# Gated delta rule: block transposes on VectorE for the inverse's transpose, and last products in runs of one shape

## The chip, the cores and the metric

The kernel runs on one core of a Trainium2 chip, whose engines work side by side and wait for each other by semaphores: TensorE (PE; its weight loads are PEld), VectorE (DVE), ScalarE (ACT), GpSimd (POOL) and SyncE (SP), which issues the loads. The metric is the device time of one execution in microseconds, as the median of the runs; lower is better.

## The reference

Two decoder blocks on 512 tokens of width 1024 (float32). The first mixes tokens in four ways at once, each with four heads of 64: softmax attention with forgetting, a gated delta rule, and two gated linear attentions; then come a feed-forward layer with a short convolution, and a second block with a convolution mixer, latent attention and two more feed-forward layers. The change lies in the gated delta rule alone, whose costly step is the solution of triangular systems, one for each head and chunk of 64 tokens:

```python
m = jnp.where(strict, jnp.einsum('bhnrd,bhnsd->bhnrs', kb, k) * decay, 0.0)
t_mat = m + jnp.eye(c, dtype=m.dtype)
w = lax.linalg.triangular_solve(t_mat, kb * jnp.exp(G)[..., None], left_side=True, lower=True, unit_diagonal=True)
u = lax.linalg.triangular_solve(t_mat, v * beta[..., None], left_side=True, lower=True, unit_diagonal=True)
```

## The kernel before

All of the first block's mixing is one stage, some 400 of 1861 us. Its dense products (29 tiles of the input projection, 8 of the output projection, each in 24 matmuls of 128x512, since every operand is split in two parts) run between four kinds of mixing work, which are written as generators in three lanes: the two linear attentions, the gated delta rule (`gdn`, once for heads 0 and 1 and once for heads 2 and 3), and softmax attention. The order of TensorE's instructions is written out by a planner, `conduct` (line 758). It keeps a clock of its own, to which each product adds a set cost (`mm`, line 704; `tr`, line 711), and resumes a generator when the time it yielded is over: `yield LV` waits 1.0 us of that clock. Where no generator is due, it issues the next step of a dense tile. The other engines take their instructions in an order that the framework derives from the program's.

`gdn` works on four chunks of 128 tokens at once (tiles of 128x512, chunk by chunk) and inverts the triangular matrices by doubling. X is the inverse so far, XT its transpose; both start from blocks of two rows. XT is made on VectorE (lines 1110 and 1111). X comes from it by four TensorE transposes into PSUM and a copy on ScalarE (line 1121, behind a `yield LV`), for each of the two heads (j). Then follow six levels (line 1125), in which the blocks grow from 2b = 4 to 128 rows. A level takes four steps, each behind a `yield LV`:

- for each head, Y = mask x (MR X): four matmuls (line 1134) and a VectorE multiplication (line 1137);
- for each head, `pp` = XT Y (line 1140), added to X on VectorE (line 1141), and `pt` = Y XT (line 1142), which a VectorE update brings into XT (line 1143). `up` and `lo` select the columns, 64 of each 128.

`mm4` makes four matmuls into one PSUM tile of the lane, and the lane has two such tiles (`gps`, line 642). Behind the levels comes one correction step (lines 1149 to 1160), and then the last products of the pair (lines 1163 to 1173): u from XT and v, w from k and XT, in 16 matmuls, of which every second has an output of 64 partitions that starts at partition 0 or 64. These are float32, so that each is two records in the profile. Two ScalarE copies bring u and w out, and a scan over the four chunks uses them.

In the rows below, TensorE's instructions stand under the lines of two helpers, 705 (matmul) and 712 (transpose), as output<-moving,stationary operand: `gps<-gx,gmr` is the Y product, `gps<-gy,gxt` is `pp`, `gps<-gxt,gy` is `pt`, `gps<-mlac,gxt` the transposes of XT, `gps<-mlac,gv` those of v, `gps<-gvn,gmr` and `gps<-gmr,gke` the last products, and `mm<-` a dense product.

Of the kernel before, what the change touches and what calls it, by code (L numbers as in the profile page):

```python
# [14 lines left out]
ACTF = mybir.ActivationFunctionType  # L15
# [630 lines left out]
LA, LV, LP = 0.68, 1.0, 1.5  # L646
# [17 lines left out]
class Mix(Mla):  # L664
# [371 lines left out]
    def gdn(self, p):  # L1036
        nc = self.nc
# [7 lines left out]
        f1 = lambda t: t.bitcast(F32)  # L1045
        G, GL = h4(self.G[:, 0:16]), h4(self.G[:, 16:32])
        eG, eGL = h4(self.eG[:, 0:16]), self.eG[:, 16:32]
        ke, ko, vn = self.b("gke"), self.b("gko"), self.b("gvn")
# [5 lines left out]
        for i, y in enumerate((k, q)):  # L1054
# [4 lines left out]
                out=ss[:, 8 - 8 * i : 16 - 8 * i], in_=sq.rearrange("p (a d) -> p a d", d=64), axis=AX.X, op=ALU.add  # L1059
# [12 lines left out]
        nk = self.s1(8, "gnk", 2)  # L1072
        nc.vector.tensor_tensor(out=nk, in0=ss[:, 8:16], in1=rr[:, 8:16], op=ALU.mult)
        yield 0.0
        MT, MR, AT, X, XT = [], [], [], [], []
        for j in range(2):
            rows = slice(64 * j, 64 * j + 64)
# [9 lines left out]
            for c in range(4):  # L1087
                nc.scalar.activation(
                    out=e[:, c * 128 : c * 128 + 128], in_=gp[:, c * 128 : c * 128 + 128], func=ACTF.Exp,
# [4 lines left out]
            for c in range(4):  # L1094
                cs = slice(c * 128, c * 128 + 128)
# [5 lines left out]
            for c in range(4):  # L1101
                cs = slice(c * 128, c * 128 + 128)
# [13 lines left out]
        tp = self.to_tokens(v)  # L1116
        nc.vector.tensor_tensor(out=d4(vn), in0=d4(tp), in1=b64(h2(nk)), op=ALU.mult)
        for j in range(2):
            yield LV
            x = self.b("gx", F32R, bufs=2)  # L1120
            nc.scalar.activation(out=x, in_=self.to_tokens(f1(XT[j])), func=ACTF.Copy)
            X.append(x)
        self.over.add(f"gdn{p}.kv")
        Y = self.gy
        for lv in range(6):
            b = 2 << lv
            up = lambda t: t.rearrange("p (n j) -> p n j", j=2 * b)[:, :, :b]
            lo = lambda t: t.rearrange("p (n j) -> p n j", j=2 * b)[:, :, b:]
            if lv == 2:
                for mt in MT:  # L1130
                    nc.gpsimd.tensor_tensor(out=c4(mt), in0=c4(mt), in1=bc(self.strict), op=ALU.mult)
            for j in range(2):
                yield LV
                yp = self.mm4(MR[j], X[j], up)
                c4b = lambda t: t.rearrange("p (c n j) -> p c n j", c=4, j=2 * b)[:, :, :, :b]
                gm = self.gmask[:, lv].rearrange("p (n j) -> p n j", j=b).unsqueeze(1).to_broadcast([128, 4, 64 // b, b])
                nc.vector.tensor_tensor(out=c4b(Y[j]), in0=c4b(yp), in1=gm, op=ALU.mult)
            for j in range(2):
                yield LV
                pp = self.mm4(XT[j], Y[j], up)  # L1140
                nc.vector.tensor_tensor(out=up(X[j]), in0=up(f1(X[j])), in1=up(pp), op=ALU.add)
                pt = self.mm4(Y[j], XT[j], lo)
                nc.vector.scalar_tensor_tensor(
                    out=lo(XT[j]), in0=lo(pt), scalar=self.grow[:, lv : lv + 1], in1=lo(f1(XT[j])),
                    op0=ALU.mult, op1=ALU.add,
                )
# [15 lines left out]
        yield LV  # L1162
        up = self.pst()
        wp = self.pst()
        for c in range(4):
            for j in range(2):
                cs = slice(c * 128, c * 128 + 128)
                hs = slice(c * 128 + j * 64, c * 128 + j * 64 + 64)
                self.mm(up[:, hs], XT[j][:, cs], vn[:, hs])
                self.mm(wp[64 * j : 64 * j + 64, cs], ke[:, hs], XT[j][:, cs])  # L1170
        u, w = vn, ke
        nc.scalar.activation(out=u, in_=up, func=ACTF.Copy)
        nc.scalar.activation(out=w, in_=wp, func=ACTF.Copy, scale=-1.0)
# [3 lines left out]
        for c in range(4):  # L1177
            cs = slice(c * 128, c * 128 + 128)
            if st is None:
                vt = u[:, cs]  # L1180
            else:
# [8 lines left out]
                    out=h64(os_[:, cs]), in0=h64(qp[:, 0:128]),  # L1190
# [3 lines left out]
            if c < 3:  # L1194
# [4 lines left out]
                for j in range(2):  # L1199
# [3 lines left out]
                    else:  # L1203
                        col = 4 * c + 2 * p + j
                        nc.vector.scalar_tensor_tensor(
                            out=new[rs, rs], in0=st[rs, rs], scalar=eGL[rs, col : col + 1], in1=kp[rs, rs],
# [4 lines left out]
            for j in range(2):  # L1211
                hs = slice(j * 64, j * 64 + 64)
# [475 lines left out]
```

## Time and profile before

| What | Value |
|---|---|
| median of the runs | 1862.54 us |
| lowest run | 1862.07 us |
| profiled execution | 1862.47 us |
| its span, first to last instruction | 1860.8 us |
| PE busy | 1822.3 us, 98% |
| PEld busy | 1501.5 us, 81% |
| DVE busy | 1050.7 us, 56% |
| ACT busy | 737.8 us, 40% |
| POOL busy | 194.4 us, 10% |

The span is the time from the first to the last instruction; the execution has some 1.7 us around it. Matmuls overlap each other in their pipeline, so that the duration of one is longer than the distance to the next; distances between starts tell what an instruction costs. PEclk is the granted share of TensorE's full clock, where 1.00 is 2.4 GHz and 0.50 is 1.2 GHz. A chain of waits is followed back from the last instruction of a stretch, at each step to what released it.

### The profile page before, as it was taken

What the parts mean: (1) busy time and instruction counts of PE and PEld (TensorE: products, weight loads), DVE (VectorE), ACT (ScalarE), POOL (GpSimd) and SP (SyncE); (2) the same over time, 40 slices, a digit from 0 to 9 for tenths busy, and PEclk for the clock granted to TensorE, in tenths of its full rate; (3) what the DMA queues carried; (4) which work ended last, traced back from release to release, by engine and by line L of the source; (5) the groups of instructions that cost most, each with busy time, mean ns of one, the idle gap of its engine ahead of it and who ended that gap; (6) DMA issues with size and microseconds to landing.
All of it is one profiled execution on the core that took longest, in us unless ns stands there. A gap on an engine that the chain in (4) does not pass through costs nothing.

```text
span 1860.8 us, 22057 instructions
## 1 busy us (share of the span) xinstructions
PE 1822.3 (98%) x8609; PEld 1501.5 (81%) x8609; DVE 1050.7 (56%) x1627; ACT 737.8 (40%) x1138; POOL 194.4 (10%) x225
## 2 busy tenths in 40 slices
PE   8999999999999999999999999999999999999997
PEld 6787887778888888888888888888777888888886
DVE  7875985767777633455564444333876454444323
ACT  6543544544444422322343233322577333232322
POOL 1510502210000001011200000011011200000001
PEclk9999999999999999999999999999999999999999
DMA  4111101332323333323232323333222222323332
GB/s 167 57 35 46 46 35 35 106 101 91 102 93 100 90 100 94 102 91 102 92 106 92 102 91 102 94 94 97 71 60 74 79 96 97 102 91 99 94 94 76
DMA packets 53223, 162.61 MB, mean 87 GB/s; under 512 B 6528, under 2 KB 13184, under 8 KB 53120
## 3 DMA queue, kind: packets, MB, share of 16 engines
q1 hardware_dynamic: 52992, 161.21, 27.2%
q8 instruction: 67, 1.10, 0.3%
q14 instruction: 36, 0.29, 0.0%
q10 hardware_dynamic: 128, 0.01, 0.0%
HBM read 157.78 MB, written 2.10 MB: 86 GB/s over the span
## 4 chain that ended last, share of the span: by engine, by line
PE 85%; DVE 9%; ACT 3%; issue 1%; POOL 1%; DMA 0%; SPq 0%; DVEq 0%; ACTq 0%; POOLq 0%
PE mm L125 24%; PE mm L127 24%; PE mm L126 24%; PE mm L705 6%; PE gps L705 3%; PE lps L705 1%; PE fps L705 1%; DVE lbd L1310 1%; ACT wh L111 1%; DVE wl L112 1%; DVE lat L1361 1%; PE ps L577 1%; DVE ptl L112 0%; PE ps L165 0%; DVE nm L580 0%
## 5 line engine op out<-in xcount | busy, mean ns | idle before, releaser
L111 ACT ACTIVATE wh<-raw 128x1024 fp32r<-128x1024 f32 (+3 forms) x308 | 308.6, 1003 | 762.6 <-PE mm L126 463.5
L125 PE MATMUL mm<-xh,wh 128*128 128x512 f32 x1336 | 521.8, 391 | 0.4 <-ACT xh L173 0.4
L126 PE MATMUL mm<-xl,wh 128*128 128x512 f32 x1336 | 520.7, 390 | 0.5 <-DVE xl L174 0.5
L127 PE MATMUL mm<-xh,wl 128*128 128x512 f32 x1336 | 519.9, 389 | 0.0
L112 DVE TENSOR_TENSOR wl<-raw,wh 128x1024 fp32r<-128x1024 f32 (+3 forms) x300 | 361.0, 1203 | 224.8 <-ACT wh L111 221.6
L126 PEld LDWEIGHTS mm<-xl,wh 128*128 128x128 f32 x1336 | 250.8, 188 | 54.9 <-DVE xl L174 1.4
L125 PEld LDWEIGHTS mm<-xh,wh 128*128 128x128 f32 x1336 | 250.8, 188 | 53.7 <-issue 1.0
L127 PEld LDWEIGHTS mm<-xh,wl 128*128 128x128 f32 x1336 | 250.8, 188 | 51.9 <-issue 0.2
L125 PE MATMUL mm<-hidh,wh 128*128 128x512 f32 (+1 forms) x614 | 236.7, 386 | 0.0
L127 PE MATMUL mm<-hidh,wl 128*128 128x512 f32 (+1 forms) x614 | 235.3, 384 | 0.0
L126 PE MATMUL mm<-hidl,wh 128*128 128x512 f32 (+1 forms) x614 | 233.8, 381 | 0.0
L127 PEld LDWEIGHTS mm<-hidh,wl 128*128 128x128 f32 x614 | 115.4, 188 | 24.2
L126 PEld LDWEIGHTS mm<-hidl,wh 128*128 128x128 f32 x614 | 115.4, 188 | 23.6
L705 PE MATMUL mm<-xh,wh 128*128 128x512 f32 x291 | 127.7, 439 | 6.6 <-ACT xh L173 5.8
L125 PEld LDWEIGHTS mm<-hidh,wh 128*128 128x128 f32 x614 | 115.5, 188 | 21.9 <-ACT wh L111 0.2
L705 PE MATMUL mm<-xh,wl 128*128 128x512 f32 x291 | 116.0, 398 | 1.6 <-DVE wl L112 1.6
L705 PE MATMUL mm<-xl,wh 128*128 128x512 f32 x291 | 116.1, 399 | 0.4 <-DVE xl L112 0.4
L278 DVE TENSOR_TENSOR u<-mm,rb 128x512 f32<-128x512 f32 x44 | 30.4, 691 | 141.2 <-PE mm L127 141.2
L158 POOL TENSOR_TENSOR z<-z,sq 128x512 f32<-128x512 f32 x31 | 50.9, 1643 | 556.6 <-ACT sq L156 518.9
L274 DVE TENSOR_TENSOR u<-mm,rb 128x512 f32<-128x512 f32 x44 | 30.4, 691 | 90.9 <-PE mm L127 90.8
L111 ACT ACTIVATE hidh<-s 128x512 fp32r<-128x512 f32 x66 | 41.8, 633 | 88.6 <-DVE s L255 57.5
L705 PEld LDWEIGHTS mm<-xh,wh 128*128 128x128 f32 x291 | 56.1, 193 | 18.8 <-ACT xh L173 6.3
(434 smaller groups left out, 2089.2 us busy)
## 6 DMA issues: line engine op xcount, KB each, us to landing
raw<-in_w_a_dram SPq DMA_DIRECT2D x52, 512.0 KB, 3.3
raw<-in_w_b_dram SPq DMA_DIRECT2D x52, 512.0 KB, 3.4
raw<-in_w_up_dram SPq DMA_DIRECT2D x44, 512.0 KB, 3.3
raw<-in_w_in_dram SPq DMA_DIRECT2D x28, 512.0 KB, 3.3
raw<-in_conv_w_in_dram SPq DMA_DIRECT2D x24, 512.0 KB, 3.3
raw<-in_w_down_dram SPq DMA_DIRECT2D x16, 448.0 KB, 3.4
raw<-in_w_a_dram SPq DMA_DIRECT2D x16, 448.0 KB, 3.3
raw<-in_w_b_dram SPq DMA_DIRECT2D x16, 448.0 KB, 3.3
```

The lines of the kernel that those rows point to most:

```text
L111: nc.scalar.activation(out=h, in_=src, func=ACTF.Copy)
L112: (eng or nc.vector).tensor_tensor(out=l, in0=src, in1=h.bitcast(F32), op=ALU.subtract)
L125: nc.tensor.matmul(out=ps, lhsT=h, rhs=xh, start=(k == 0), stop=False)
L126: nc.tensor.matmul(out=ps, lhsT=h, rhs=xl, start=False, stop=False)
L127: nc.tensor.matmul(out=ps, lhsT=l, rhs=xh, start=False, stop=(k == kt - 1))
L158: eng.tensor_tensor(out=acc, in0=acc, in1=sq, op=ALU.add)
L274: nc.vector.tensor_tensor(out=g, in0=ps, in1=r, op=ALU.mult)
L278: nc.vector.tensor_tensor(out=g, in0=ps, in1=r, op=ALU.mult)
L577: nc.tensor.matmul(out=ps[:, :n], lhsT=l[:, qs], rhs=r[:, :n], start=(i == 0), stop=False)
L705: self.nc.tensor.matmul(out=out, lhsT=lhsT, rhs=rhs, start=start, stop=stop)
L1310: nc.vector.tensor_tensor(out=bd[rows, :, h].rearrange("p c (n j) -> p c n j", j=b), in0=c4(q)[rows], in1=c4(d)[rows], op=ALU.mult)
L1361: nc.vector.copy_predicated(out=at.rearrange("p c (n j) -> p c n j", j=2 * b)[:, :, :, b:], mask=self.lmask[:, lv - 1].rearrange("p (n j) ...
```

## The change

Three edits, all in `gdn`. The first X of each head comes from XT by a VectorE transpose of the whole 128x512 tile and a ScalarE copy that rounds it; the yields before it go. This transpose turns each 32x32 block within itself, which is the transpose of a matrix that has nothing outside its diagonal blocks of up to 32 rows. In the levels with 2b up to 32, the first four of six, the same helper makes XT from the new X, in place of the product `pt` and its update; the last two levels stay. The last products are issued as eight for u and then eight for w.

```diff
@@ -1072,6 +1072,12 @@
         nk = self.s1(8, "gnk", 2)
         nc.vector.tensor_tensor(out=nk, in0=ss[:, 8:16], in1=rr[:, 8:16], op=ALU.mult)
         yield 0.0
+        def flipped(dst, src):
+
+            t = self.t(tag="s")
+            nc.vector.transpose(out=t, in_=f1(src))
+            nc.scalar.activation(out=dst, in_=t, func=ACTF.Copy)
+
         MT, MR, AT, X, XT = [], [], [], [], []
@@ -1116,9 +1122,8 @@
         tp = self.to_tokens(v)
         nc.vector.tensor_tensor(out=d4(vn), in0=d4(tp), in1=b64(h2(nk)), op=ALU.mult)
         for j in range(2):
-            yield LV
             x = self.b("gx", F32R, bufs=2)
-            nc.scalar.activation(out=x, in_=self.to_tokens(f1(XT[j])), func=ACTF.Copy)
+            flipped(x, XT[j])
             X.append(x)
@@ -1139,6 +1144,10 @@
                 yield LV
                 pp = self.mm4(XT[j], Y[j], up)
                 nc.vector.tensor_tensor(out=up(X[j]), in0=up(f1(X[j])), in1=up(pp), op=ALU.add)
+                if 2 * b <= 32:
+
+                    flipped(XT[j], X[j])
+                    continue
                 pt = self.mm4(Y[j], XT[j], lo)
@@ -1162,12 +1171,14 @@
         yield LV
         up = self.pst()
         wp = self.pst()
-        for c in range(4):
-            for j in range(2):
-                cs = slice(c * 128, c * 128 + 128)
-                hs = slice(c * 128 + j * 64, c * 128 + j * 64 + 64)
-                self.mm(up[:, hs], XT[j][:, cs], vn[:, hs])
-                self.mm(wp[64 * j : 64 * j + 64, cs], ke[:, hs], XT[j][:, cs])
+        blocks = [
+            (slice(c * 128, c * 128 + 128), slice(c * 128 + j * 64, c * 128 + j * 64 + 64), j)
+            for c in range(4) for j in range(2)
+        ]
+        for cs, hs, j in blocks:
+            self.mm(up[:, hs], XT[j][:, cs], vn[:, hs])
+        for cs, hs, j in blocks:
+            self.mm(wp[64 * j : 64 * j + 64, cs], ke[:, hs], XT[j][:, cs])
```

## Rows read from the trace of the kernel before

**Rows 1.** The page, first section: busy time, share of span, instructions of each engine

```profile
PE 1822.3 (98%) x8609; PEld 1501.5 (81%) x8609; DVE 1050.7 (56%) x1627; ACT 737.8 (40%) x1138; POOL 194.4 (10%) x225
```

**Rows 2.** Stretches: length; busy us (instructions) of PE, PEld, DVE, ACT, POOL; PEclk, DMA, GB/s

```profile
0.00:400.00 400.00, 378.88 (x2095) 311.22 (x2096) 293.49 (x630) 195.55 (x381) 97.89 (x110) 0.99 0.21 68
110.50:114.00 3.50, 3.50 (x12) 2.89 (x11) 3.47 (x6) 1.78 (x2) 0.00 (x0) 0.53 0.00 0
291.00:298.00 7.00, 6.40 (x22) 5.22 (x23) 4.98 (x9) 6.30 (x10) 4.79 (x5) 0.54 0.24 76
```

**Rows 3.** Chain of waits, shares by line: 79 to 122, 230 to 276, 180 to 240 us

```profile
by line: PE mm L705 39.5%; PE gps L705 21.2%; PE lps L705 15.0%; DVE lat L1361 6.3%; DVE fq L1442 3.5%; DVE sq L145 3.0%; PE fps L705 3.0%; DVE sq L143 2.6%; DVE sq L142 2.4%; DVE gxt L1143 0.9%; DVE gy L1137 0.8%; PE lps L712 0.8%; DVE gx 
by line: PE mm L705 28.0%; PE gps L705 14.2%; PE lps L705 7.2%; DVE lat L1361 5.6%; DVE lst L1401 4.6%; DVE lbd L1310 4.4%; PE fps L705 3.8%; issue 3.7%; DVE fq L1442 3.2%; DVE fk L1442 3.2%; DVE sq L145 3.0%; DVE sq L142 3.0%; DVE sq L143 
by line: DVE lbd L1310 18.7%; DVE lat L1361 12.4%; issue 8.9%; POOL s L1299 5.1%; DVE wl L112 5.1%; PE lps L705 3.7%; DVE gq L228 3.5%; DVE gmt L1031 3.4%; DVE gat L1031 3.4%; DVE lg L1338 2.3%; ACT L264 2.1%; DVE gate L927 2.0%; DVE gxt L1
```

**Rows 4.** Timeline of PE: start us, us, line, operation, count; second product and a transpose

```profile
76.08 0.60 PE L712 MATMUL gps<-mlac,gxt 128*128 128x128 f32 x4
76.44 0.48 PE L705 MATMUL mm<-xh,wh 128*128 128x512 f32 x1
...
83.82 0.53 PE L705 MATMUL gps<-gy,gxt 128*128 128x64 f32 x4
84.18 0.62 PE L705 MATMUL gps<-gxt,gy 128*128 128x64 f32 x4
84.62 0.48 PE L705 MATMUL mm<-xh,wh 128*128 128x512 f32 x1
```

**Rows 5.** Groups by line, 60 to 400 us: count | busy us, mean ns | idle before

```profile
L705 PE MATMUL gps<-gxt,gy 128*128 128x64 f32 x96 | 15.3, 284 | 2.2 <-DVE gxt L1143 1.9 <-DVE gy L1137 0.3
L1143 DVE SCALAR_TENSOR_TENSOR gxt<-gps,grow,gxt 128x256 fp32r<-128x256 f32 x24 | 11.4, 476 | 0.4 <-PE gps L705 0.2
L1107 ACT ACTIVATE gmr<-gmt 128x512 fp32r<-128x512 f32 x4 | 2.5, 628 | 2.6 <-DVE gmt L1031 2.6
L1110 DVE TENSOR_TENSOR u<-gmt,mixb 128x512 f32<-128x512 f32 x4 | 2.7, 680 | 0.0
L1341 DVE TENSOR_TENSOR_SCAN lf<-resets,lf 128x512 f32<-128x512 bf16 x2 | 3.3, 1632 | 0.0
L1257 DVE TENSOR_SCALAR lf<-lf,lb 128x512 f32<-128x512 f32 x1 | 0.5, 547 | 0.1
```

**Rows 6.** Timeline of PE: last products of the second pair, and a run of one shape

```profile
305.94 0.33 PE L705 MATMUL gps<-gvn,gmr 128*128 128x64 f32 x2
306.20 0.43 PE L705 MATMUL gps<-gmr,gke 128*64 128x128 f32 x2
...
311.65 0.50 PE L705 MATMUL mm<-xh,wh 128*128 128x512 f32 x1
315.17 1.06 PE L705 MATMUL fps<-fv,fpt 128*128 128x64 f32 x8
316.06 0.39 PE L712 MATMUL lps<-mlac,lv 128*128 128x128 f32 x2
```

**Rows 7.** Waits of PE, 60 to 400 us: us in total, times, longest

```profile
PE gps L705 <- DVE gxt L1143: 1.9, 4, 0.6
PE gps L705 <- DVE gx L1141: 1.5, 2, 1.0
```

**Rows 8.** Timeline of PE: a product that waits, in the second pair's last level

```profile
291.60 1.06 PE L705 MATMUL gps<-gxt,gy 128*128 128x64 f32 x4 [0.60 <-DVE gxt L1143]
```

**Rows 9.** Timeline of PE and DVE around the first X of the second pair

```profile
224.87 0.60 PE L712 MATMUL gps<-mlac,gv 128*128 128x128 f32 x4
226.71 0.60 PE L712 MATMUL gps<-mlac,gxt 128*128 128x128 f32 x4
230.51 0.72 PE L705 MATMUL gps<-gx,gmr 128*128 128x64 f32 x4
230.52 0.69 DVE L1117 TENSOR_TENSOR gvn<-gps,gnk 128x512 f32<-128x512 f32 x1
```

## The prediction

> **What bounds the kernel now.** I read the page first. TensorE is busy for 98% of the span and VectorE for 56% [rows 1], so the first question is whether TensorE is also what ends last where the change acts. The table of stretches splits the span: the mixing stage takes the first 400 us, the feed-forward and attention stages the rest of 1860.8. The change touches only the mixing stage, and in it only the gated delta rule, which runs twice (heads 0 and 1, then heads 2 and 3). In the stage TensorE is busy for 379 of 400 us and VectorE for 293 [rows 2]: both are near full, and a saving on one can be eaten by the other. So I read the chain of waits in three stretches. From 79 to 122 us, levels 0 to 3 of the first pair, 39.5 + 21.2 + 15.0 = 76% of the chain is TensorE. From 230 to 276 us, the same levels of the second pair, the TensorE entries add to 28.0 + 14.2 + 7.2 + 3.8 = 53%. From 180 to 240 us, which leads into the second pair, the chain is mostly VectorE [rows 3]. So TensorE sets the pace around the first pair, VectorE ahead of the second, and the two share it inside the second.
>
> **What TensorE loses.** In levels 0 to 3 the second product (`pt`, line 1142) goes: 4 levels x 2 heads x 2 pairs = 16 groups of four matmuls, 64 of the 96 in the row [rows 5]. One group stands in the timeline: `pp` starts at 83.82, `pt` at 84.18 and the next dense matmul at 84.62, so that `pt` holds the engine for 0.44 us [rows 4]. 16 x 0.44 = 7.0 us. The four groups of transposes that made the first X go too. One runs from 76.08 until the next matmul at 76.44, 0.36 us [rows 4]; 4 x 0.36 = 1.4 us.
>
> The last products keep their 32 records in each pair, and only their order changes. Now two records of one shape alternate with two of the other, from 305.94 until the next matmul at 311.65: 5.71 us, or 0.71 for each of the eight pairs of shapes. A run of one shape is far denser: eight records of the 128x64 kind take 316.06 - 315.17 = 0.89 us, 0.11 each [rows 6]. By that, two runs of 16 take 3.56 us. Four records without a change of shape would take 0.44 us where 0.71 are seen, so that a change costs about 0.135 us; with two left, the new order takes 3.83 us and saves 1.88 us in each pair of heads, 3.8 us in all.
>
> In the second run the output still alternates between partitions 0 and 64, and the trace of before never shows that without a change of shape between. If each of the 15 changes of position cost the 0.135 us of a change of shape, 2.0 us would be lost and the order would gain nothing; if short weight loads ran at half the price of a record, 0.9 us more would be won. I take 1.88 as the value between, since one shape is kept. The Trainium skill (TensorEngine Tiling (Array Packing), Key Properties) says that a change of tiling mode drains the engine and that a change of the tile within a mode doesn't. By that rule the 1.88 us stands; were it wrong for positions, the order would gain nothing, and the sum below would be 3.8 us worse.
>
> TensorE is thus freed of 7.0 + 1.4 + 3.8 = 12.2 us, in each pair 4.2 around the levels and 1.88 at the end. Weighted by the chain's TensorE share, the first pair gives 0.76 x 4.2 + 1.88 = 5.1 us and the second 0.53 x 4.2 + 1.88 = 4.1 us. The last products I count in full, as their stretch from 305.94 is TensorE's alone with nothing waited for in the rows [rows 6]. **Landing: -9.2 us.**
>
> **Waits that go.** The lane has two PSUM tiles. A level rotates `pp`, `pt` of one head and `pp`, `pt` of the other through them, so that a product waits until VectorE has read the one before last: 1.9 us for `gxt` at line 1143 and 1.5 us for `gx` at line 1141 [rows 7]. Without `pt`, each `pp` needs a tile that was read a step earlier. **-3.4 us.** The clock is tied to this. In the stretch from 110.5 to 114 us the granted clock is 0.53 and from 291 to 298 us 0.54, nearly all at the lower level of 1.2 GHz, where the whole stage has 0.99 [rows 2]. These cost 3.5 x 0.47 + 7.0 x 0.46 = 4.9 us. The second one sets in right at such a wait, at 291.60 us [rows 8]; but TensorE waits for other things there too, so I take half. **-2.4 us.**
>
> **What VectorE and ScalarE gain.** VectorE drops 16 updates of 0.476 us (line 1143) and adds 20 block transposes of 128x512: 16 in the levels and 4 for the first X. The trace has no such instruction. The lowest row with that width is a one-source scalar operation from SBUF, 0.547 us, the highest the scan, 1.63 us; the common one, from line 1110, is 0.680 us [rows 5]. I take 0.68, since a transpose reads one operand once and carries nothing from element to element. Net: 20 x 0.68 - 16 x 0.476 = +6.0 us; by the bounds +3.3 and +25 us. Weighted by what isn't TensorE in the chain, it costs 0.24 x 3.0 + 0.47 x 3.0 = **+2.1 us**. ScalarE gets 16 more copies of 0.628 us [rows 5], 10.0 us. These are hidden: ScalarE is busy for 195 of 400 us [rows 2], and XT isn't read until the next level's `pp`, four steps later, while in the timeline one step takes about 2 us (224.87, 226.71, and two more to 230.51) [rows 9]. If the cover is gone, up to 10 us show.
>
> **The wait that is new.** Two steps of the planner go (the `yield` at line 1119), so the first product of level 0 is issued two steps earlier, and the first X now comes over VectorE and ScalarE. In the second pair VectorE runs behind: the transposes of v start at 224.87 and take 0.60, but the VectorE instruction that reads them starts only at 230.52 [rows 9]. The two new transposes queue behind it. X of the second head is then there at 230.52 + 0.69 + 2 x 0.68 + 0.63 = 233.2 us, X of the first at about 232.5, while TensorE reaches the first product at about 226.7, not 230.5. It could stand for 5.8 us, with the dense products and the other lanes queued behind it. But VectorE has 5 us of work in hand at that time and is what the chain runs through, so TensorE's standing costs less than it shows. Lower bound nothing, upper 5.8 and an estimated 1 in the first pair, where the chain shows no such lag; I take **+3.0 us** together.
>
> Earlier release of the key and value buffers (line 1123) costs and saves nothing that I can price: the planner puts some dense tiles two steps earlier, and the dense work fills the same holes. The order of TensorE is worked out anew from the planner's clock, so everything after a pair shifts; I allow 5 us either way for it.
>
> **Sum.** -9.2 - 3.4 - 2.4 + 2.1 + 3.0 = -9.9 us. The profiled execution took 1862.47 us, of which 1860.8 are its span, and the median of the runs is 1862.54, so the two bases agree. 1862.5 - 9.9 = **1853 us**, with its own range of 1847 to 1858. Chance 0.45.
>
> **Rivals.** *All of it lands.* TensorE really is the bound, both slow-clock stretches vanish and the new wait is covered: -12.2 - 3.4 - 4.9 = -20.5, **1842 us**. For it: TensorE's 98%. Against: the chain from 180 to 240 us [rows 3]. Chance 0.2.
>
> *VectorE takes over, slower.* Place: the VectorE queue from 224 us through the levels of the second pair. TensorE's 8.4 us around the levels become slack, VectorE's +6.0 land in full, and so do 5.8 + 1.0 us of waiting for the first X; only the 3.8 us of the last products are kept: 6.0 + 6.8 - 3.8 = +9.0, **1872 us**. It decides where 9.9 us more land than in my sum: all of VectorE's with a transpose of 0.68 + 9.9 / 20 = 1.2 us, or a new XT that is late by 9.9 / 16 = 0.6 us at each of its uses. For it: VectorE's backlog of 5 us [rows 9]. Against: 76% of TensorE in the first pair's chain [rows 3]. The Trainium skill (TensorE: Matmul & The Clock Gate, Architectural detail) says that ScalarE and VectorE take their queues strictly in order; by that rule a copy to XT that waits for its transpose also holds the weight copies behind it, and it speaks for this case. Chance 0.15.
>
> *Nothing moves.* The saving goes into slack and the new order of TensorE gives back the rest: within 3 us of before, **1862 us**. For it: both engines are near full. Chance 0.2.
>
> **Range.** From 1842 to 1867: it leaves out some of the first rival, where the gain is still larger (0.07), and most of the second (0.12). A change of 2%, about what a measurement of this kernel can tell from no change, is 37 us. No case reaches it but by the scan's price for a transpose together with late copies: faster 0.01, within 0.97, slower 0.02.
>
> **What would show it.** The 128x64 row of `pt` falls from 96 to 32 and the transposes of gxt leave TensorE. A VectorE row of 20 transposes appears; at 0.68 us the sum stands, at 1.2 us the slower rival does. The last products of a pair take 3.8 us, not 5.7. The waits of TensorE for gx and gxt on VectorE shrink, and a wait for gx on ScalarE of a few microseconds appears once in each pair. The stretches at the lower clock shorten. The feed-forward stage starts some 10 us earlier and keeps its pace. I am wrong if the stage ends as before although these counts hold: then another engine's chain sets its end.

## The result, and the profile after

| Kernel | median | ratio to before, 95% interval |
|---|---|---|
| before | 1862.5 us | |
| after | 1876.8 us | 1.0078 [1.0063, 1.0092] |

The change makes the kernel slower by 14 us, where 9.9 us less were forecast; the range ended at 1867. One more execution of each kernel, of 4696.7 and 3281.8 us, was in a slow state and is left out of the medians. The page of the changed kernel, its span and first section:

```profile
span 1874.5 us, 21932 instructions
...
PE 1817.9 (97%) x8529; PEld 1497.0 (80%) x8529; DVE 1061.8 (57%) x1631; ACT 748.5 (40%) x1154; POOL 194.4 (10%) x225
```

The counts came as forecast: 80 matmul records fewer on TensorE (64 of the second products, 16 transposes), VectorE +4 instructions, ScalarE +16. TensorE is busy for 4.4 us less [rows 1], and yet the span is 13.7 us longer: TensorE stands still for 1874.5 - 1817.9 = 56.6 us, where it was 1860.8 - 1822.3 = 38.5.

The table of stretches tells where. I cut it at the first feed-forward matmul, which ends the mixing stage (columns as in [rows 2]); first before, then after:

```profile
0.00:399.50 399.50, 378.38 (x2093) 310.95 (x2094) 292.99 (x629) 195.05 (x380) 97.89 (x110) 0.99 0.21 68
```

```profile
0.00:410.30 410.30, 373.31 (x2013) 306.42 (x2014) 301.97 (x632) 203.54 (x392) 96.53 (x109) 0.97 0.20 66
```

The stage is 10.8 us longer, and what follows 2.9 us. Inside the stage TensorE's busy time falls by only 5.1 us, where 12.2 were counted, at a granted clock of 0.97 and not 0.99; its idle time rises from 21.1 to 37.0 us. Idle time and clock ate the saving, and more.

The groups by line, 60 to 420 us, after (to be compared with [rows 5]):

```profile
L1078 DVE STREAM_TRANSPOSE u<-gx 128x512 f32<-128x512 f32 x16 | 11.3, 707 | 0.4
L1079 ACT ACTIVATE gxt<-u 128x512 fp32r<-128x512 f32 x16 | 10.0, 627 | 20.3 <-DVE u L1078 20.3
L705 PE MATMUL gps<-gxt,gy 128*128 128x64 f32 x32 | 4.9, 277 | 0.7 <-DVE gy L1142 0.7
...
L1078 DVE STREAM_TRANSPOSE u<-gxt 128x512 f32<-128x512 f32 x4 | 2.6, 680 | 0.0
```

A block transpose of 128x512 takes 0.68 to 0.71 us; 0.68 was assumed. The second products are down from 96 to 32. So no operation costs more than forecast. The waits of TensorE, 60 to 420 us, after (us in total, times, longest; to be compared with [rows 7]):

```profile
PE gps L705 <- ACT gx L1079: 6.7, 2, 3.5
PE fps L705 <- ACT fpt L1486: 4.3, 1, 4.3
PE fps L705 <- ACT sq L1446: 4.0, 2, 2.7
PE mm L705 <- ACT xh L111: 2.9, 1, 2.9
PE gps L705 <- ACT gko L1062: 2.3, 1, 2.3
PE mm L126 <- DVE xl L174: 2.1, 3, 0.9
```

Before, the longest line of this list was 1.9 us [rows 7]. Only the first of the new ones, the wait for the first X, is on the path that was edited. `fpt` and `sq` belong to softmax attention, `xh` feeds dense products, and `gko` is made in `gdn` ahead of the edit. The edits change none of them, only the order in which TensorE asks for them. All four are made on ScalarE, which has new copies in its queue, so that either could be the cause; the runs below part them.

The first X of the second pair, in the timelines of PE, DVE and ACT (to be compared with [rows 9]):

```profile
229.62 0.40 PE L705 MATMUL mm<-xh,wl 128*128 128x512 f32 x1
233.55 1.06 PE L705 MATMUL gps<-gx,gmr 128*128 128x64 f32 x4 [3.53 <-ACT gx L1079]
234.42 0.77 PE L705 MATMUL mm<-xh,wh 128*128 128x512 f32 x1
234.99 0.63 PE L705 MATMUL mm<-xl,wh 128*128 128x512 f32 x1
235.42 0.63 PE L705 MATMUL mm<-xh,wl 128*128 128x512 f32 x1
...
231.54 0.68 DVE L1123 TENSOR_TENSOR gvn<-gps,gnk 128x512 f32<-128x512 f32 x1
232.14 1.28 DVE L1078 STREAM_TRANSPOSE u<-gxt 128x512 f32<-128x512 f32 x2
...
232.86 1.22 ACT L1079 ACTIVATE gx<-u 128x512 fp32r<-128x512 f32 x2 [3.02 <-DVE u L1078]
```

This is the wait that was forecast: the transposes stand behind `gvn` in VectorE's queue, and TensorE, whose next instruction is that product, stands for 3.53 us. The lines behind it show the second cost: the dense matmuls then start 0.43 us apart, where they start 0.23 us apart in the stage's other stretches. The windows behind five such waits, after:

```profile
80.00:84.00 4.00, 4.00 (x16) 3.44 (x17) 0.43 (x1) 0.44 (x1) 0.00 (x0) 0.58 0.04 17
...
107.00:110.50 3.50, 3.05 (x7) 1.91 (x8) 3.42 (x7) 1.69 (x4) 0.00 (x0) 0.54 0.00 0
...
234.00:238.00 4.00, 4.00 (x14) 3.42 (x15) 2.19 (x7) 0.08 (x1) 0.00 (x0) 0.50 0.00 0
...
305.00:310.00 5.00, 4.16 (x15) 3.78 (x16) 1.80 (x6) 3.38 (x10) 1.91 (x3) 0.53 0.11 44
...
364.00:370.00 6.00, 6.00 (x27) 5.00 (x27) 3.67 (x5) 0.00 (x0) 0.00 (x0) 0.78 0.35 124
```

The waits end at 79.90 (3.17 us, for gx), 107.45 (2.72, sq), 233.55 (3.53, gx), 305.84 (4.29, fpt) and 361.52 (2.88, xh). Behind the first four, the granted clock is at or near its lower level of 1.2 GHz for a few microseconds (0.50 to 0.58); the last window is at that level for about half of its 6 us. There is a sixth such stretch, from 206.7 to 210.1 us at 0.56, behind the wait of 2.3 us for `gko`. Of the two stretches that were slow before [rows 2], that from 291 to 298 us is now at 1.00, and that from 110.5 to 114 at 0.97.

### The profile page after: what moved, and what is told of

The parts are those of the page before. It is cut to its first block, busy times and chain, and to the rows that moved or that the text cites. A ratio compares the mean times of both kernels' runs of the same rounds, so it can differ in the third digit from the quotient of the medians.

```text
span 1874.5 us, 21932 instructions
## 1 busy us (share of the span) xinstructions
PE 1817.9 (97%) x8529; PEld 1497.0 (80%) x8529; DVE 1061.8 (57%) x1631; ACT 748.5 (40%) x1154; POOL 194.4 (10%) x225
## 4 chain that ended last, share of the span: by engine, by line
PE 83%; DVE 9%; ACT 4%; issue 1%; POOL 1%; DMA 0%; SPq 0%; DVEq 0%; POOLq 0%; ACTq 0%
PE mm L125 24%; PE mm L127 24%; PE mm L126 24%; PE mm L705 6%; PE gps L705 2%; PE lps L705 1%; PE fps L705 1%; DVE wl L112 1%; DVE lbd L1321 1%; ACT wh L111 1%; POOL s L1310 1%; DVE lat L1372 0%; PE ps L577 0%; DVE xl L112 0%; PE ps L165 0%
```

## The experiments

Each run lists span and granted clock, so that its span parts into what the clock took (span x (1 - clock), to 0.9 us because of the clock's rounding) and the rest. Not all of the first part is a loss: in the trace of before, the last 9.8 us are at 0.52 and hold no TensorE instruction, which makes 4.7 us of the 7.9, and every trace ends in such a way. Differences between kernels are what counts. The table gives their means over the runs, and, from each one's profiled execution, where the mixing stage ends, and TensorE's idle time in it. "New order" says which edits are let into the planner's clock; with "old", the planner is charged for a removed product as if it were still there, so that the order of TensorE's remaining instructions is that of before. The runs fall in several sessions, and before was measured in each: its median was 1861.0 to 1862.5. All differences are below 2%, and are read against the intervals.

| Kernel | Work changed | TensorE's order | median | ratio, 95% | clock took | rest | stage ends | idle in it |
|---|---|---|---|---|---|---|---|---|
| before | none | old | 1861.0 to 1862.5 | | 7.9 | 1852.4 | 399.5 | 21.1 |
| after | X, levels, last | new | 1876.8 | [1.0063, 1.0092] | 18.7 | 1856.1 | 410.3 | 37.0 |
| e1_runs | last | old | 1857.6 | [0.9961, 0.9983] | 7.8 | 1847.5 | 395.5 | 23.3 |
| e2_first_x | X | new, X | 1880.2 | [1.0084, 1.0116] | 15.5 | 1863.2 | 417.6 | 37.4 |
| e3_levels | levels | new, levels | 1881.9 | [1.0092, 1.0123] | 28.2 | 1851.5 | 419.2 | 31.6 |
| e4_yields | X, levels, last | new, levels | 1871.9 | [1.0034, 1.0074] | 21.0 | 1848.8 | 411.1 | 32.6 |
| e5_old_plan | X, levels, last | old | 1855.7 | [0.9956, 0.9995] | 13.9 | 1842.1 | 401.7 | 27.5 |
| e6_x_by_tensore | levels, last | new, levels | 1868.9 | [1.0008, 1.0039] | 16.6 | 1847.4 | 398.0 | 31.0 |
| e7_x_old_plan | levels, last | old | 1852.5 | [0.9941, 0.9968] | 8.2 | 1843.5 | 388.8 | 25.9 |
| e8_twice | as e5, each transpose twice | old | 1867.2 | [1.0025, 1.0054] | 18.2 | 1848.6 | 402.8 | 32.2 |
| e9_first_x_old_plan | X | old | 1864.0 | [1.0001, 1.0020] | 8.9 | 1853.3 | 401.5 | 24.4 |
| e10_order | none | new, levels | 1875.4 | [1.0057, 1.0088] | 14.1 | 1859.5 | 413.3 | 32.6 |
| e11b_order_x | none | new, X | 1875.2 | [1.0056, 1.0092] | 12.6 | 1860.9 | 413.4 | 32.9 |
| e11_order_all | last | new, X and levels | 1875.4 | [1.0049, 1.0092] | 13.6 | 1859.7 | 408.8 | 34.1 |

Executions of one kernel differ by what the clock took: e5_old_plan's from 9.3 to 20.5 us, with times of 1853.7 to 1865.2, and its profiled execution is the longest. e6_x_by_tensore's ten fall into two groups, four of 1858.5 to 1863.2 us and six of 1868.9 to 1869.8, and its profiled execution (1861.2) is of the first, so that its stage end isn't that of its median. So I read the rest beside the median.

### The three edits, each alone

e1_runs takes the last edit only:

```diff
-                self.mm(up[:, hs], XT[j][:, cs], vn[:, hs])
-                self.mm(wp[64 * j : 64 * j + 64, cs], ke[:, hs], XT[j][:, cs])
+        for cs, hs, j in blocks:
+            self.mm(up[:, hs], XT[j][:, cs], vn[:, hs])
+        for cs, hs, j in blocks:
+            self.mm(wp[64 * j : 64 * j + 64, cs], ke[:, hs], XT[j][:, cs])
```

> The kernel before with the last products in runs of one shape and nothing else. All theories: the 32 records of a pair take 3.83 us instead of 5.71, TensorE's order is otherwise the same, so 3.8 us faster, about 1859 us. If a change of output position costs as much as a change of shape: no change.

The last products of its second pair, in the timeline of PE:

```profile
304.83 1.89 PE L705 MATMUL gps<-gvn,gmr 128*128 128x64 f32 x16
306.65 1.09 PE L705 MATMUL gps<-gmr,gke 128*64 128x128 f32 x16
307.68 0.50 PE L705 MATMUL mm<-xh,wh 128*128 128x512 f32 x1
```

They take 307.68 - 304.83 = 2.85 us, where 3.83 were forecast and 5.71 stood before [rows 6]: 2.86 us less in each pair, 5.7 in all. The kernel is faster by 0.28%, 5.2 us (3.4 by the medians of the session, 4.9 in the rest); the interval is 3.2 to 7.3 us. So most of it lands, and all of it may.

e2_first_x takes the first edit only:

```diff
-            yield LV
             x = self.b("gx", F32R, bufs=2)
-            nc.scalar.activation(out=x, in_=self.to_tokens(f1(XT[j])), func=ACTF.Copy)
+            flipped(x, XT[j])
```

> The kernel before with the first X by VectorE and ScalarE and without the two yields, and nothing else. Theory 'early product' (the first product of level 0 stands in TensorE's order before its X is there): two waits of 3 to 4 us for gx from ScalarE, each followed by a stretch at the lower clock, 8 to 12 us slower than before, 1870 to 1874 us. Theory 'VectorE' (its extra work sets the end): only 4 x 0.68 us are added and 1.4 us of TensorE go, so within 2 us of before.

It costs 18 us by itself, more than either theory gave, although TensorE has 1.4 us less to do. Its waits of TensorE, 60 to 420 us:

```profile
PE gps L705 <- ACT gx L1079: 8.8, 2, 5.7
PE fps L705 <- ACT fpt L1480: 5.0, 2, 3.6
```

e3_levels takes the second edit only:

```diff
+                if 2 * b <= 32:
+                    flipped(XT[j], X[j])
+                    continue
                 pt = self.mm4(Y[j], XT[j], lo)
```

> The kernel before with XT by transposes in the first four levels, first X as before. Theory 'early product': the loss isn't here, 7 us of TensorE go and 3.3 us of VectorE come, 1855 to 1860 us. Theory 'VectorE': 3.3 us of VectorE and 10 us of ScalarE land, 1864 us or more. Theory 'order' (the planner's new order of TensorE is worse): anything, with new waits in lanes other than the delta rule's.

It costs 20 us by itself. Its rest, 1851.5, is that of before, and its clock takes 28.2 us. One stretch of its trace:

```profile
300.00:340.00 40.00, 38.47 (x160) 29.66 (x159) 15.28 (x31) 11.22 (x27) 8.33 (x8) 0.62 0.04 14
```

From 300 to 340 us TensorE is busy for 38.5 of 40 us and does its work at a granted clock of 0.62. For 30.7 us of it, from 306.8 on, the clock is at 0.50 while TensorE is busy throughout (30.7 us); the waits just ahead are of 1.25 and 0.28 us. Why the clock stays low for so long isn't shown. So two of three edits that take work from TensorE are slower alone. Either the way over VectorE and ScalarE costs this, or the order that the planner makes of the shorter program.

### The same work in the old order

e5_old_plan is the changed kernel with the yields at the first X back, and the planner's clock charged for what is gone:

```diff
+            yield LV
+            self.clk += 4 * 0.108
             x = self.b("gx", F32R, bufs=2)
             flipped(x, XT[j])
...
                     flipped(XT[j], X[j])
+                    self.clk += 4 * 0.08
                     continue
```

> The changed kernel with the two yields back and the planner's clock charged for the removed products and transposes, so that TensorE's order is that of before with only the removed instructions missing. Theory 'early product' and theory 'order': both causes are gone, TensorE's 12 us count, 1850 to 1857 us. Theory 'VectorE': its 6 us and ScalarE's 10 us are all still there, 1862 us or more.

e4_yields has the first two of these lines but not the charge in the levels.

> The changed kernel with the two yields back and the clock charged for the missing transposes of the first X; the levels' missing product stays uncharged, so that the planner still makes a new order from level 0 on. Theory 'early product': most of the loss goes, since the first product of level 0 is back in its place, 1857 to 1862 us. Theory 'order': the new order behind it is what costs, 1868 to 1880 us.

With the same work on the same engines, the old order takes 1855.7 us, the changed kernel's 1876.8, and the order with only the levels uncharged 1871.9. The order is thus worth 16 to 21 us, and what the three edits move between the engines is a gain of 0.25%. The early first product, which e4_yields takes back, is 5 us of the 21 at most.

e6_x_by_tensore is the changed kernel without the first edit, e7_x_old_plan the same with the levels charged:

```diff
+            yield LV
             x = self.b("gx", F32R, bufs=2)
-            flipped(x, XT[j])
+            nc.scalar.activation(out=x, in_=self.to_tokens(f1(XT[j])), func=ACTF.Copy)
...
                     flipped(XT[j], X[j])
+                    self.clk += 4 * 0.08     # e7_x_old_plan alone
                     continue
```

> The changed kernel with the first X by TensorE transposes as before, with their yields; levels and last products as changed, uncharged. It is the levels-only kernel plus the last products in runs. Theory 'early product': nothing early is left, 1853 to 1858 us. Theory 'order': the levels-only kernel less 4 us, 1876 to 1879 us, with about 1% of the clock lost.

> First X by TensorE as before, XT by block transposes in four levels with the planner's clock charged for the missing product, last products in runs: TensorE's order is that of before without the 16 products. Theory 'order': 1846 to 1854 us, the best of all, as the wait for the first X on ScalarE (3.5 us in the old-order kernel) goes and only 1.4 us of TensorE come back. Theory 'VectorE': no better than 1856 us, since 16 of the 20 transposes and all 16 copies are still there.

Again 16 us lie between the two orders by the medians, 13 by the means, since e6_x_by_tensore's executions fall into two groups; "order" had put it at 1876 to 1879. e7_x_old_plan beats both kernels: 1852.5 us, ratio 0.9955 [0.9941, 0.9968]. Its stage:

```profile
0.00:388.80 388.80, 362.94 (x2029) 300.27 (x2030) 296.86 (x629) 204.21 (x396) 98.37 (x110) 0.99 0.21 70
```

Against before, TensorE's busy time falls by 15.4 us and its idle time rises by 4.8, so that the stage ends 10.7 us earlier. This is the forecast's own mechanism, and near its size, at a clock of 0.99, for two of the three edits.

### How much VectorE bears

e8_twice is e5_old_plan with the transpose in `flipped` written twice:

```diff
             nc.vector.transpose(out=t, in_=f1(src))
+            nc.vector.transpose(out=t, in_=f1(src))
```

> The old-order kernel with each block transpose issued twice into the same tile: 20 x 0.7 = 14 us more on VectorE, the same results, TensorE's order unchanged. Theory 'VectorE' (its work lands in full): 1868 to 1870 us. Theory 'order': most of it is hidden or shows as a longer wait for the first X only, 1857 to 1863 us.

```profile
L1078 DVE STREAM_TRANSPOSE u<-gx 128x512 f32<-128x512 f32 x16 | 11.2, 702 | 0.2
L1079 DVE STREAM_TRANSPOSE u<-gx 128x512 f32<-128x512 f32 x16 | 11.2, 702 | 0.1
```

The 20 added transposes are 13.9 us of VectorE, and the kernel takes 11.5 us more than e5_old_plan, of which 6.5 are in the rest. That is above what "order" gave and just under "VectorE": VectorE's work on this path isn't hidden, as the rival of the VectorE queue had it. (Each new XT also comes 0.7 us later, and the run doesn't part the two.) But at that rate the 6 us that the change adds there cost about 3 to 5 us, and the change does not lose 14 us by it, since e5_old_plan holds all of that work and is faster than before.

### The order without the work

The last four runs part the two causes from the other side. e9_first_x_old_plan is before with the first X over VectorE and ScalarE in the old order; it differs from e2_first_x only in `yield LV` and `self.clk += 4 * 0.108`, as in e5_old_plan.

> The kernel before with the first X made by VectorE and ScalarE, but the yields stay and the planner's clock is charged what the transposes on TensorE were worth, so that TensorE's order is that of before without these transposes. If the early first product made the edit cost its 18 us (1880.2 without the yields), this one stays near before, 1858 to 1865 us. If the path of the first X over VectorE and ScalarE is what costs, whatever the order, 1872 us or more.

1864.0 us: 16 us less than e2_first_x, and about 1.7 more than before. The first product still waits for X (3.26 us in the second pair, in the timeline), and the stage ends 2.0 us later. That is the price of the way itself.

In e10_order all work stays on its engines; only the planner doesn't count the second products of levels 0 to 3:

```diff
                 pt = self.mm4(Y[j], XT[j], lo)
+                if 2 * b <= 32:
+                    self.clk -= 4 * 0.08
```

> The kernel before with all its work on the engines where it was; only the planner's clock isn't charged for the second products of levels 0 to 3 (the 16 groups of four), so that the order of TensorE's other instructions becomes that of the kernel in which only the levels were changed (1881.9 us). If the order is what costs there, 1873 to 1888 us, with waits and lower-clock stretches at other places than before. If the transposes on VectorE cost it, 1858 to 1866 us.

e11b_order_x does the same at the first X, and e11_order_all does both, with the last products in runs:

```diff
         for j in range(2):
-            yield LV
             x = self.b("gx", F32R, bufs=2)
             nc.scalar.activation(out=x, in_=self.to_tokens(f1(XT[j])), func=ACTF.Copy)
+            self.clk -= 4 * 0.108
```

> The kernel before without the yields at the first X and with its TensorE transposes kept out of the planner's clock: the order of TensorE of the kernel in which only the first X was changed (1880.2 us), but X by TensorE and ScalarE. If the path over VectorE makes that order costly (its first product waits 3.2 and 5.7 us for X), 1858 to 1867 us. If the order alone costs, 1873 to 1885 us.

> The order of TensorE of the changed kernel with the work where it was before: first X by TensorE's transposes and second products in all levels, both kept out of the planner's clock, no yields at the first X; last products in runs. If the order costs and the removed 8.4 us of TensorE are a gain, 1873 to 1890 us. If VectorE's and ScalarE's new work is what made the changed kernel slower, 1855 to 1864 us.

All three are slower than before by 0.7%, with no block transpose in them. e11_order_all shows the changed kernel's waits for `xh`, `fpt` and `gko`, although ScalarE has none of the new copies:

```profile
PE mm L705 <- ACT xh L111: 2.9, 1, 2.9
PE fps L705 <- ACT fpt L1479: 2.5, 1, 2.5
PE gps L705 <- ACT gko L1062: 2.3, 1, 2.3
PE fps L705 <- ACT sq L1439: 0.9, 1, 0.9
```

Of the 13.5 us that the changed kernel waits for these four, 8.6 are here; the other 4.9, for `sq` and `fpt`, came only with the work moved as well. The stage of e10_order, and the waits of its TensorE, 60 to 420 us:

```profile
0.00:413.30 413.30, 380.69 (x2094) 312.34 (x2095) 299.91 (x631) 196.29 (x381) 96.35 (x110) 0.98 0.20 67
```

```profile
PE gps L705 <- DVE gx L1141: 5.0, 4, 2.0
PE lps L705 <- DVE lat L1363: 3.2, 2, 1.9
PE fps L705 <- ACT fpt L1477: 2.5, 1, 2.5
PE gps L705 <- ACT gko L1062: 2.2, 1, 2.2
```

TensorE's work is that of before to within a record (378.4 and 380.7 us busy), but it stands still for 32.6 us and not 21.1, and the stage ends 13.8 us later. The waits are for `fpt` (softmax attention) and `gko`, as in the changed kernel, for `lat` (a linear attention; 1.7 us before), and for the levels' own X. The other engines' order is derived from the same program, so that these runs show what the new order of the whole costs, not TensorE's share in it. The same work in two orders, in medians:

| Work | old order | new order | the order costs |
|---|---|---|---|
| that of before | 1862.3 | 1875.4 (levels), 1875.2 (X) | 13, 13 |
| with last products in runs | 1857.6 | 1875.4 (both) | 18 |
| with the first X by VectorE | 1864.0 | 1880.2 (X) | 16 |
| levels by VectorE, last in runs | 1852.5 | 1868.9 (levels) | 16 |
| all three edits | 1855.7 | 1871.9 (levels), 1876.8 (both) | 16, 21 |

Seven comparisons, five kinds of work: the order costs 13 to 21 us in each by medians (13 to 18 by means), whoever makes the transposes.

## Why the prediction was wrong

**TensorE's saving: right, in the old order.** The step counted 12.2 us freed, of which 9.2 land. (The first pair's share of 76% leaves out the `fps` entry of 3.0% that the second's counts; that is 0.1 us.) In the trace of after, 16 second products and four groups of transposes are gone, and the last products take 2.85 us a pair where 3.83 were forecast. In the old order these land: the last products 3.4 to 5.2 us (e1_runs, by medians and by ratio), and together with the levels 8.4 to 9.8 (e7_x_old_plan, by ratio and by medians), where 12.7 us of TensorE are gone and VectorE has some 4 us more. The term of the last products was mis-sized on the safe side: its price per record, 0.11 us, holds for the u products (16 in 1.82 us), but the 16 w products take 1.03 us until the next matmul, 0.06 each. The output's change between partitions 0 and 64, for which a cost was feared, shows none. What came instead is the forecast's own upper case, short weight loads at half the price, 0.9 us more; it was 0.98. The weight loads of u and w in e1_runs:

```profile
304.60 1.98 PEld L705 LDWEIGHTS gps<-gvn,gmr 128*128 128x128 f32 x16
306.65 0.85 PEld L705 LDWEIGHTS gps<-gmr,gke 128*64 128x64 f32 x16
```

Those of w have half the columns, and 16 take less than half as long. The Trainium skill (TensorEngine Tiling (Array Packing), Key Properties) says that a change of tile within a mode doesn't drain the engine, and also that different tiles can load weights and multiply in parallel. This trace agrees with the first by its 0.06 us for each record; whether tiles overlapped here isn't shown, since the shorter loads give the same number.

**Waits that go: right in place, eaten by others.** The waits for `gxt` and `gx` on VectorE (3.4 us [rows 7]) are gone from the list of after, and 0.9 us is left of them in e7_x_old_plan. But TensorE's idle time in that kernel's stage is 4.8 us longer than before, since other waits came (3.0 us for `lst` and 2.2 for `gate`, two tiles of other lanes).

**VectorE and ScalarE: right in size, too low in what lands.** A transpose takes 0.68 to 0.71 us, against 0.68. Of the added 6.0 us, 2.1 were taken to land, by the chain's shares; at e8_twice's rate (6.5 to 11.5 of 13.9 us) it is about 3 to 5. The ScalarE copies are not on the path in e7_x_old_plan, which has all 16 of them in the levels and is the fastest kernel.

**The new wait: right in place, wrong in what hangs on it.** Up to 5.8 us were forecast for the second pair and 1 for the first; 3.53 and 3.17 came. But +3.0 was taken, on the reasoning that TensorE's standing costs less than it shows because VectorE had work in hand. In the old order that is about so: e9_first_x_old_plan loses 1.7 us to before and e5_old_plan 3.2 to e7_x_old_plan. With the yields gone the same edit costs 18 (e2_first_x).

**The clock: wrong in sign.** The step took half of the two slow stretches as a gain, -2.4 us. Those two did go, but six others came behind new waits, and what the clock took rose from 7.9 to 18.7 us. This alone is 10.8 of the 14.5 us by which the mean span grew.

**The planner's order: the step that failed.** "The order of TensorE is worked out anew from the planner's clock, so everything after a pair shifts; I allow 5 us either way for it." It stood at nothing in the sum. It is worth 21 us in this kernel (e5_old_plan against after), and 13 to 18 us where it was changed with no work moved. With the order kept, all three edits give 1855.7 us, within the 1847 to 1858 that the sum allowed. TensorE is busy for 95% of the stage [rows 2] and takes its matmuls in the order that the planner wrote: in the timeline above, the product that waits 3.53 us for the first X stops the dense products behind it. The forecast saw this for the one product whose yields it read in the diff, and priced the other moves by a guess that rested on no row. Those others turned out to be the larger part: the waits for `fpt`, `sq`, `xh` and `gko` sum to 13.5 us in the list above, against 6.7 for the first X, and none of these four is made by a line of the diff.

**The rivals.** *Nothing moves* named the mechanism, a new order of TensorE that gives back the saving, but only at the saving's size, 1862. The slower one had the sign, 1872, and e8_twice confirms its premise that VectorE's time isn't hidden here. But its mechanism, VectorE's added work landing in full, isn't what made the changed kernel slower: that work is in e5_old_plan too, and e10_order, e11b_order_x and e11_order_all are as slow without it. The Trainium skill (TensorE: Matmul & The Clock Gate, Architectural detail) was cited for it, that ScalarE takes its queue strictly in order. ScalarE did stand for 20.3 us ahead of the sixteen copies in after, as the row of L1079 shows, but in e7_x_old_plan it also stands, for 11.5 us, and that kernel is the fastest.

**What stays open.** Why the new orders are worse is shown only as far as the waits go. All the new orders tried were slower than the old one, but they are few and of one family (steps of `gdn` earlier on the planner's clock), so that whether another order would beat the old one wasn't tried. How much of the order's cost is the waits and how much the clock can't be parted exactly, and it differs: in e10_order and e11b_order_x the clock took 5 to 6 us more than before and the rest grew by 7 to 9; after against e5_old_plan it is 4.8 and 14.0, and e6_x_by_tensore against e7_x_old_plan 8.4 and 3.9.

## What to carry to other kernels

In this kernel, the order cost more than the work saved. Where a written-out order is made by a planner that counts the work, an edit that removes work is two edits: less work, and another order for everything behind it. Cost them apart: first keep the order (charge the planner for what is gone) and measure the work, then let the order go and measure that. On an engine that is busy for 95% and takes its work in a fixed order, look in the trace after for waits on operands that the diff never names, and for the clock behind them.

## What the runs showed of the hardware

- Behind each of five waits of TensorE of 2.7 to 4.3 us the granted clock was 0.50 to 0.78 in the 3.5 to 6 us read there, in a kernel where TensorE is busy for 97%. It also fell behind a wait of 0.60 us (291.60, before [rows 8]), and in e3_levels it stood at 0.50 for 30.7 us with TensorE busy throughout. What the clock takes differs between executions of one kernel (9.3 to 20.5 us in e5_old_plan) and accounts for most of their spread.
- Sixteen float32 records with 64-partition outputs that alternate between partitions 0 and 64 take 1.03 us as one run, 16 with outputs of 128 partitions 1.82 us; their weight loads take 0.85 and 1.98 us. Alternating with each other in twos, all 32 take 5.71 us [rows 6].
- A VectorE block transpose of 128x512 in float32 takes 0.68 to 0.71 us, as much as a tensor-tensor operation of that shape [rows 5].
